# Instruction order at three places of a two-layer trunk, and a root kept in PSUM

## The chip, the cores and the metric

The kernel runs on one core of a Trainium2 chip. The core has a matrix engine (TensorE, PE), a vector engine (VectorE, DVE), a scalar engine (ScalarE, ACT), a general engine (GpSimd, POOL) and an engine that only issues transfers (SyncE, SP). Each works through a queue of its own in order, and they meet at semaphores. The metric is the device time of one execution in microseconds, as the median of several runs.

## The reference

Two layers are applied to 1024 prompt frames and 32 sample frames of width 1024, all in float32. Each layer has a recurrent mixer and a feed-forward part with a convolution over three frames; layer 0 has retention, layer 1 has gated linear attention (GLA).

```python
def rmsnorm(x, g):
    y = x * lax.rsqrt(jnp.mean(x * x, axis=-1, keepdims=True) + EPS)
    return y * g

def gla_chunk(S, xs):                  # q, k, v and the log decay lg of a chunk
    b = jnp.cumsum(lg, axis=1)
    expo = where(causal, b[:, :, None] - b[:, None, :], -inf)
    A = einsum('bihd,bjhd,bijhd->bhij', q, k, exp(expo))
    intra = einsum('bhij,bjhe->bihe', A, v)
    cross = einsum('bihd,bhde->bihe', q * exp(b), S)
    S_new = exp(bL) * S + einsum('bjhd,bjhe->bhde', k * exp(bL - b), v)

def gla_mixer(h, S0, w_in, w_a2, b_a, norm_g, w_out):
    q, k, v, r, a = split(h @ w_in)    # a: 16 decay features per frame
    lg = log_sigmoid(a @ w_a2 + b_a) / GLA_TAU
    ...
    return (silu(r) * o) @ w_out

def conv_ffn(h, conv_state, w_up, conv_w, conv_b, w_down):
    u = h @ w_up                       # 2 * 2816 columns
    c = conv_b + sum(ext[:, j:j + T] * conv_w[j] for j in range(3))
    gate, val = split(c)
    return (silu(gate) * val) @ w_down

def trunk(x, ...):
    for i in range(2):
        x = x + mixer_i(rmsnorm(x, norm_mix[i]))
        x = x + conv_ffn(rmsnorm(x, norm_ffn[i]))
    return rmsnorm(x, norm_final)      # and the new states
```

## The kernel before

**Products.** Features lie on the 128 partitions (eight tiles `kt`), the 1056 frames along the columns. A float32 product is made of three TensorE matmuls: the operand is split into a high part and the rest, and high x high, high x rest and rest x high are added in PSUM. `load_w` (L103) does this for a weight tile of 128x1024: a transfer into `raw`, a cast by ScalarE to `whi`, and a subtraction by VectorE to `wlo` (both at L110). `raw` has three buffers, so the next load waits for these two. `split_x` (L160) does it for the activations: ScalarE writes `xh` (XA in the trace, L162), VectorE `xl` (L163).

**The down projection**, the class `Down7`, works on 22 tiles of the 2816 columns in windows. The frames are in two halves `s` of 528 columns, each of two blocks of 264 (TH). A 2x2 block product is made with seven products instead of eight (`product`; ORD is the order of the seven, and L1703 to L1705 are the three matmuls of a term). VectorE adds each result from its PSUM tile `pu` into the residual `AR`: at L1784 after the seven products, at L1720 for the last windows, which are plain (`plain_product`). A PSUM tile can be written again only after these adds. The four row groups `p` of the residual become final one after the other.

**Behind the last windows.** In layer 0 `new_squares` adds the squares of the new residual into R (L1811), `new_x` splits it into `xh` and `xl` with the gain of the next norm and stores it, and `rms_a` and `rms_b` make the root of the mean for one chunk of columns: a matmul with ones gives the sums (`pn`, L189), ScalarE takes Ln and Exp, VectorE does a Newton step (L177 to L179) and writes the diagonal matrix `dg` (L196), and a matmul of `dg` with ones spreads the result over the partitions (`pr`, L202), from where ScalarE copies it into R. In layer 1 `squares`, `row`, `root` and `out` do the final norm for blocks (s, half): `row` sums the squares on TensorE (L1842) and issues Ln, Exp and a square on ScalarE, `root` is the Newton step on VectorE (L1853 to L1855), and four `out` per block multiply the residual by R (L1860) and store it.

**The GLA** has four heads and three chunks of 384, 384 and 288 columns. `gates_in(c)` makes the decay features, `qk_products` the products with the weights of q and k, `qk_out` scales them, `gate` makes the scan b along the columns, `weigh` the exponentials x at seven levels (GpSimd subtracts at L1116, ScalarE takes Exp, VectorE multiplies by k and q at L1122 and L1123). `scores` makes the mask A (L1171) and the scores (L1180), and `mix` the values with the weights `w_gv`, whose rest part is `vl` (L1262).

**What sets the order.** A scheduler places the instructions of each engine from the order of the calls and the waits; `order(a, b)` forces a behind b. The tables `ends` and `news` in `run` say behind which product (window, half, index) the steps of the end are called.

## Time and profile before

| | |
|---|---|
| Median of 3 timed runs | 2796.37 us (2794.09 to 2799.51) |
| The profiled execution | 2787.05 us, span 2785.3 us |
| Mean granted TensorE clock in it | 0.997 |
| TensorE busy | 2733.5 us, 98% |
| VectorE busy | 2047.1 us, 73% |
| ScalarE busy | 1370.3 us, 49% |
| GpSimd busy | 402.7 us, 14% |

The span is the time from the first to the last instruction of the execution; start times in the timelines count from its start. Busy time of an engine says nothing of what it holds up; that is read from the waits and the timeline. The end of layer 0 lies at about 1560 to 1585 us, the first scores of the GLA at 1622 us and the end of layer 1 behind 2757 us.

### The profile page before, as it was taken

How to read it: one execution, taken by the hardware profiler on the slowest of the kernel's cores; microseconds unless marked ns; L12 is line 12 of the kernel's file. 1: busy time of each engine (PE TensorE's matmuls, PEld its weight loads, DVE VectorE, ACT ScalarE, POOL GpSimd, SP SyncE). 2: the span in 40 equal slices, each digit the busy share in tenths (PEclk: the TensorE clock that was granted, in tenths of full speed). 3: DMA queues.
4: the chain of work that ended last, by engine and by line, in shares of the span. 5: the costliest groups of instructions: out<-in, count | busy, mean ns of one | idle time of the engine just before them, and what ended most of it. 6: DMA issues, size and time to landing. Idle time of an engine off the chain costs nothing.

```text
span 2785.3 us, 55419 instructions
## 1 busy us (share of the span) xinstructions
PE 2733.5 (98%) x22272; PEld 2644.8 (95%) x22272; DVE 2047.1 (73%) x3558; ACT 1370.3 (49%) x2520; POOL 402.7 (14%) x672
## 2 busy tenths in 40 slices
PE   9999999999999999999999889999999999999997
PEld 9999988888999999999999889999999999999997
DVE  7876666766557988888876777775379888888666
ACT  7444354444435544444544466664255444446445
POOL 0000000000112211111211232220132111112113
PEclk9999999999999999999999999999999999999999
DMA  6233455554875343323988411115532442329883
GB/s 241 87 115 102 137 157 139 160 143 117 287 252 186 118 141 124 104 96 111 299 200 227 147 32 53 54 46 199 184 128 93 138 141 101 108 82 306 200 223 115
DMA packets 276241, 410.30 MB, mean 147 GB/s; under 512 B 56784, under 2 KB 208976, under 8 KB 270864
## 3 DMA queue, kind: packets, MB, share of 16 engines
q1 hardware_dynamic: 257184, 347.88, 38.4%
q0 software_dynamic: 18256, 58.35, 8.8%
q8 instruction: 174, 2.85, 0.4%
q14 instruction: 83, 0.68, 0.1%
q10 hardware_dynamic: 544, 0.54, 0.1%
HBM read 264.49 MB, written 142.21 MB: 146 GB/s over the span
## 4 chain that ended last, share of the span: by engine, by line
PE 81%; DVE 7%; ACT 3%; DMA 3%; POOL 2%; issue 2%; SPq 0%; DVEq 0%; ACTq 0%; POOLq 0%
PE pu L436 13%; PE pu L431 13%; PE pu L435 13%; PE pu L1703 4%; PE pu L1704 4%; PE pu L1705 4%; PE pd L1513 2%; PE pd L1511 2%; PE pd L1512 2%; PE psv L265 2%; PE psv L266 2%; PE psv L267 2%; POOL x L1116 2%; PE pg L133 1%; PE pg L134 1%
## 5 line engine op out<-in xcount | busy, mean ns | idle before, releaser
L410 ACT COPY HR<-pu 128x264 f32<-128x264 f32 x264 | 98.7, 375 | 257.8 <-PE pu L436 251.8
L436 PE MATMUL pu<-XA,wgl 128*128 128x264 f32 x752 | 213.4, 284 | 0.0
L431 PE MATMUL pu<-XA,wgh 128*128 128x264 f32 x752 | 212.8, 283 | 0.0
L435 PE MATMUL pu<-XA,wgh 128*128 128x264 f32 x752 | 212.5, 283 | 0.0
L1987 DVE SCALAR_TENSOR_TENSOR AR<-AR,cw 128x1058 f32<-128x1058 f32 x88 | 115.9, 1319 | 70.8 <-ACT AR L1986 63.3
L1960 DVE TENSOR_TENSOR AR<-HR,pu 128x264 f32<-128x264 f32 (+2 forms) x440 | 144.2, 369 | 5.6 <-ACT HR L410 3.7
L431 PEld LDWEIGHTS pu<-XA,wgh 128*128 128x128 f32 x752 | 141.2, 188 | 0.3 <-ACT wgh L367 0.3
L435 PEld LDWEIGHTS pu<-XA,wgh 128*128 128x128 f32 x752 | 141.2, 188 | 0.0
L436 PEld LDWEIGHTS pu<-XA,wgl 128*128 128x128 f32 x752 | 141.0, 188 | 0.0
L431 PE MATMUL pu<-XA,wsh 128*128 128x264 f32 x464 | 132.5, 286 | 2.3 <-ACT HR L410 1.2
L436 PE MATMUL pu<-XA,wtl 128*128 128x264 f32 x464 | 131.9, 284 | 0.0
L436 PE MATMUL pu<-XA,wsl 128*128 128x264 f32 x464 | 131.8, 284 | 0.0
L431 PE MATMUL pu<-XA,wth 128*128 128x264 f32 x464 | 131.6, 284 | 0.0
L435 PE MATMUL pu<-XA,wsh 128*128 128x264 f32 x464 | 131.4, 283 | 0.0
L435 PE MATMUL pu<-XA,wth 128*128 128x264 f32 x464 | 131.1, 283 | 0.0
L1984 POOL COPY cst<-AR 128x2 f32<-128x2 f32 x88 | 49.8, 566 | 562.3 <-DVE AR L1960 562.3
L1986 ACT ACTIVATE AR<-AR,cw 128x1058 f32<-128x1058 f32 x88 | 111.8, 1273 | 12.2 <-DVE AR L1960 11.1
L1988 DVE SCALAR_TENSOR_TENSOR AR<-AR,cw 128x1058 f32<-128x1058 f32 x88 | 115.6, 1316 | 0.0
L110 DVE TENSOR_TENSOR wlo<-raw,whi 128x1024 fp32r<-128x1024 f32 x74 | 93.1, 1262 | 28.2 <-ACT whi L110 21.8
L110 ACT CAST whi<-raw 128x1024 fp32r<-128x1024 f32 x74 | 77.0, 1049 | 59.7 <-PE pg L134 25.3
L368 DVE TENSOR_TENSOR wtl<-rv,wth 128x1024 fp32r<-128x1024 f32 x58 | 70.9, 1223 | 41.3 <-ACT wth L367 41.0
L436 PE MATMUL pu<-XB,wtl 128*128 128x264 f32 x352 | 100.5, 286 | 0.0
(667 smaller groups left out, 11060.9 us busy)
## 6 DMA issues: line engine op xcount, KB each, us to landing
scr_h<-AR SPq DMA_DIRECT2D x162, 264.0 KB, 2.5
scr_x<-AR POOLq DMA_DIRECT2D x88, 264.0 KB, 6.7
rg<-w_up SPq DMA_DIRECT2D x44, 512.0 KB, 3.8
rv<-w_up SPq DMA_DIRECT2D x44, 512.0 KB, 3.6
raw<-w_ro SPq DMA_DIRECT2D x39, 512.0 KB, 5.8
XA<-scr_h SPq DMA_DIRECT2D x64, 264.0 KB, 5.0
AR<-scr_x SPq DMA_DIRECT2D x12, 1056.0 KB, 7.1
scr_hr<-hl SPq DMA_DIRECT2D x20, 512.0 KB, 4.1
```

The lines of the kernel that those rows point to most:

```text
L110: ins = S.copy(hi, raw), V.tensor_tensor(lo, raw, hi.bitcast(F32), op=ALU.subtract)
L410: ins = S.copy(t, b)
L431: mm = PE.matmul(ps, wh[:, k], x[:, 0, kt], start=m in (1, 2, 4, 5) and kt == 0, stop=False, skip_group_check=True)
L435: PE.matmul(ps, wh[:, k], x[:, 1, kt], start=False, stop=False, skip_group_check=True)
L436: mm = PE.matmul(ps, wl[:, k], x[:, 0, kt], start=False, stop=kt == 3, skip_group_check=True)
L1703: PE.matmul(ps, wh, x[:, 0], start=first, stop=False, skip_group_check=True)
L1704: PE.matmul(ps, wh, x[:, 1], start=False, stop=False, skip_group_check=True)
L1705: return PE.matmul(ps, wl, x[:, 0], start=False, stop=last, skip_group_check=True)
L1960: last_put[0] = V.tensor_tensor(u[:, d:d + n], t[:, o:o + n], b[:, o:o + n], op=op)
L1986: S.activation(cj, uj[:, 2:T + 4], AF.Identity, scale=cw[:, nt, 2:3], bias=cw[:, nt, 3:4])
L1987: V.scalar_tensor_tensor(cj, uj[:, 1:T + 3], cw[:, nt, 1:2], cj, op0=ALU.mult, op1=ALU.add)
L1988: V.scalar_tensor_tensor(cj, uj[:, 0:T + 2], cw[:, nt, 0:1], cj, op0=ALU.mult, op1=ALU.add)
```

## The change

It has three parts.

1. **End of layer 0, second half.** The weights `w_gqk` of the first head are loaded by a new method `ahead`, whose VectorE step is ordered behind the last add into the residual (`self.put`). The splits `new_x` of three row groups are called behind the last product and ordered behind that add as well. The root of chunk 0 is called at other products; `dg` and its product with ones are replaced by three matmuls of the root, broadcast along the columns, with the identity.
2. **Start of the GLA.** `gates_in` is cut in two (`gates_in`, `gates_out`) and uses the PSUM tag "lv". The sums of chunk 1 are called between the q and the k product of head 0, the roots of chunks 1 and 2 and the features follow in another order. The VectorE step of the first `w_gv` is ordered behind the features of chunk 2.
3. **End of layer 1.** `row` of block (1, 0) is called behind the last product. `root` writes its result over the PSUM tile, ScalarE copies it to R except for the last block, and `out` reads the PSUM tile on VectorE and R on GpSimd. One more `out` goes to GpSimd.

```diff
@@ -157,11 +157,13 @@
 
-    def split_x(idx, src, kt, c0, n):
+    def split_x(idx, src, kt, c0, n, after=None):
         g = gcol[:, idx, kt:kt + 1]
         ins = S.activation(xh[:, kt, c0:c0 + n], src, AF.Copy, scale=g)
-        V.scalar_tensor_tensor(xl[:, kt, c0:c0 + n], src, g, xh[:, kt, c0:c0 + n].bitcast(F32),
-                               op0=ALU.mult, op1=ALU.subtract)
+        lo = V.scalar_tensor_tensor(xl[:, kt, c0:c0 + n], src, g, xh[:, kt, c0:c0 + n].bitcast(F32),
+                                    op0=ALU.mult, op1=ALU.subtract)
+        if after is not None:
+            order(lo, after)
@@ -191,15 +193,20 @@
         V.tensor_scalar(m_, ps[:, 0:3], 1.0 / D, EPS, op0=ALU.mult, op1=ALU.add)
-        rsqrt(r_, t_, m_)
-        dg = nps[0].tile([P, 3, P], F32, tag="dg", name=f"dg{i}", bufs=1)
-        V.tensor_tensor(dg, ident.unsqueeze(1).to_broadcast([P, 3, P]),
-                        r_.unsqueeze(2).to_broadcast([P, 3, P]), op=ALU.mult)
-        return dg
-
-    def rms_b(dg, c, ps):
+        for ins in (S.activation(t_, m_, AF.Ln), S.activation(r_, t_, AF.Exp, scale=-0.5)):
+            order(ins, table[0])
+        return r_, t_, m_
+
+    def newton(r_, t_, m_):
+        V.tensor_tensor(t_, r_, r_, op=ALU.mult)
+        V.scalar_tensor_tensor(t_, t_, -0.5, m_, op0=ALU.mult, op1=ALU.mult)
+        return V.scalar_tensor_tensor(r_, t_, 1.5, r_, op0=ALU.add, op1=ALU.mult)
+
+    def rms_b(c, ps):
         c0, n = CM[c]
-        PE.matmul(ps[:, :n], ones, dg.rearrange("p m t -> p (m t)")[:, :n], start=True, stop=True)
+        for m, (o, _, L) in enumerate(minors(c)):
+            PE.matmul(ps[:, o:o + L], rc[:, 3 * c + m:3 * c + m + 1].to_broadcast([P, P]), ident[:, :L],
+                      start=True, stop=True)
@@ -1054,7 +1061,7 @@
 
-        def qk_products(h, c):
+        def qk_products(h, c, between=None):
@@ -1062,6 +1069,8 @@
             proj(pq[:, :n], wq[h], c0, n)
+            if between:
+                between()
@@ -1218,7 +1227,7 @@
             if c == 0:
-                wv[h] = [load_w(io["w_gv"][h, t], None, (None, second_mask[0])) for t in range(2)]
+                wv[h] = [load_w(io["w_gv"][h, t], None, (None, second_mask[0] or features[2])) for t in range(2)]
@@ -1345,10 +1354,14 @@
             c0, n = CM[c]
-            ps = pp.tile([P, 512], F32, tag="pj", name=f"pa{c0}", bufs=2)
+            ps = lv("pa")
             for kt in range(KT):
                 PE.matmul(ps[:32, :n], wa[:, kt], xh[:, kt, c0:c0 + n], start=kt == 0, stop=False)
                 PE.matmul(ps[:32, :n], wa[:, kt], xl[:, kt, c0:c0 + n], start=False, stop=kt == KT - 1)
+            return ps
+
+        def gates_out(c, ps):
+            c0, n = CM[c]
@@ -1357,18 +1370,26 @@
 
-        gates_in(0)
-        p00 = qk_products(0, 0)
+        def mean(c):
+            return rms_a(c, pp.tile([P, GDV], F32, tag="v", name=f"pn{uid()}", bufs=2))
+
+        g00 = gates_in(0)
+        mid = []
+        p00 = qk_products(0, 0, lambda: (gates_out(0, g00), mid.append(mean(1))))
+        newton(*mid[0])
         q00 = qk_out(0, p00)
+        rms_b(1, lv("pr"))
+        mid = mean(2)
         b00 = gate(0, 0)
-        for c in (1, 2):
-            rms_b(rms_a(c, lv("pn")), c, lv("pr"))
+        g01 = gates_in(1)
+        newton(*mid)
+        rms_b(2, lv("pr"))
+        gates_out(1, g01)
+        gates_out(2, gates_in(2))
         for f in closers:
             f()
         g2 = es.enter_context(pool("g2", side="right"))
         units = [(h, c) for h in range(GH) for c in range(3)]
-        gates_in(1)
-        gates_in(2)
@@ -1717,7 +1738,7 @@
                 y = self.Y[p][:, tile, t0 + half * TH:t0 + half * TH + TH]
-                V.tensor_tensor(y, y, ps, op=ALU.add)
+                self.put = V.tensor_tensor(y, y, ps, op=ALU.add)
@@ -1766,6 +1787,10 @@
 
+        def ahead(self, j):
+            k = self.nxt[j]
+            ahead[k] = load_w(io[k[0]][k[1:]], None, (None, self.put))
+
@@ -1814,7 +1839,7 @@
             for j in range(2):
-                split_x(2, y[:, j], 2 * p + j, t0, n)
+                split_x(2, y[:, j], 2 * p + j, t0, n, self.put if s else None)
@@ -1846,18 +1871,21 @@
                 order(ins, table[0])
-            self.rows[s, half] = m_, t_, r_, ps
+            self.rows[s, half] = ps, m_, t_, r_
 
         def root(self, s, half):
-            m_, t_, r_, ps = self.rows.pop((s, half))
+            ps, m_, t_, r_ = self.rows[s, half]
             V.tensor_scalar(m_, ps, 1.0 / D, EPS, op0=ALU.mult, op1=ALU.add)
             V.scalar_tensor_tensor(t_, t_, -0.5, m_, op0=ALU.mult, op1=ALU.mult)
-            V.scalar_tensor_tensor(r_, t_, 1.5, r_, op0=ALU.add, op1=ALU.mult)
+            V.scalar_tensor_tensor(ps, t_, 1.5, r_, op0=ALU.add, op1=ALU.mult)
+            if not (s and half):
+                S.copy(r_, ps)
 
         def out(self, s, half, q, eng=V):
             t0, n = 2 * TH * s + TH * half, TH
             y = self.Y[q][:, :, t0:t0 + n]
-            eng.tensor_tensor(y, y, R[:, t0:t0 + n].unsqueeze(1).to_broadcast([P, 2, n]), op=ALU.mult)
+            r = R[:, t0:t0 + n] if eng is G else self.rows[s, half][0]
+            eng.tensor_tensor(y, y, r.unsqueeze(1).to_broadcast([P, 2, n]), op=ALU.mult)
@@ -1887,19 +1915,19 @@
             got = {}
-            row, root, out = self.row, self.root, self.out
+            row, root, out, root_of = self.row, self.root, self.out, newton
             ends = {(0, 1): [(row, 0, 0)], (0, 2): [(root, 0, 0)], (0, 3): [(out, 0, 0, 3, G), (out, 0, 0, 0), (row, 0, 1)],
                     (0, 4): [(out, 0, 0, 1), (root, 0, 1)], (0, 5): [(out, 0, 0, 2)],
                     (0, 6): [(out, 0, 1, 3, G), (out, 0, 1, 0)], (1, 0): [(out, 0, 1, 1)], (1, 1): [(out, 0, 1, 2)],
-                    (1, 3): [(row, 1, 0)],
-                    (2, 3): [(root, 1, 0), (row, 1, 1)] + [(out, 1, 0, q) for q in (3, 0, 1, 2)]
+                    (2, 3): [(row, 1, 0), (root, 1, 0), (row, 1, 1), (out, 1, 0, 3, G)] + [(out, 1, 0, q) for q in range(3)]
                     + [(root, 1, 1)] + [(out, 1, 1, q) for q in (3, 0, 1, 2)]}
             new = self.new_x
-            dg = []
+            mean = []
             news = {(0, 0, 0): [(self.consts,)], (1, 0, 1): [(new, 3, 0)], (1, 0, 3): [(new, 0, 0)], (2, 0, 1): [(new, 1, 0)],
-                    (0, 1, 0): [(new, 2, 0)], (0, 1, 3): [(lambda: dg.append(rms_a(0, self.sm("pn"))),)],
-                    (0, 1, 5): [(lambda: rms_b(dg[0], 0, self.sm("pr")),)], (1, 1, 0): [(preload, *self.nxt)],
-                    (1, 1, 1): [(new, 3, 1)], (1, 1, 3): [(new, 0, 1)], (2, 1, 1): [(new, 1, 1)], (2, 1, 3): [(new, 2, 1)]}
+                    (0, 1, 0): [(new, 2, 0)], (0, 1, 2): [(lambda: mean.append(rms_a(0, self.sm("pn"))),)],
+                    (0, 1, 4): [(lambda: root_of(*mean[0]),)], (0, 1, 6): [(lambda: rms_b(0, self.sm("pr")),)],
+                    (1, 1, 0): [(self.ahead, 0)], (1, 1, 1): [(new, 3, 1)], (1, 1, 2): [(self.ahead, 1)],
+                    (2, 1, 3): [(new, 0, 1), (new, 1, 1), (new, 2, 1)]}
```

**VectorE, end of layer 0.** The rows around the first add from pu983, product 3 of the second half; pu981 and pu982 hold products before it, pu987 and on the plain windows at the end, wlo988 to wlo991 the rests of `w_gqk`. Before:

```order
L110 TENSOR_TENSOR wlo989_17466<-raw989_17463,whi989_17465 128x1024
L177 TENSOR_TENSOR tm985_17396<-rc_66 128x3
L1784 TENSOR_TENSOR AR0_7514<-AR0_7514,pu981_17345 128x528
L178 SCALAR_TENSOR_TENSOR tm985_17396<-tm985_17396 128x3
L163 SCALAR_TENSOR_TENSOR XA_64<-AR0_7514,gcol_67,XA_64 128x528
L179 SCALAR_TENSOR_TENSOR rc_66<-tm985_17396,rc_66 128x3
L1784 TENSOR_TENSOR AR0_7514<-AR0_7514,pu983_17372 128x264
```

After:

```order
L1809 TENSOR_TENSOR AR0_7514<-AR0_7514,pu982_17361 128x264
L1809 TENSOR_TENSOR AR0_7514<-AR0_7514,pu981_17345 128x528
L1809 TENSOR_TENSOR AR0_7514<-AR0_7514,pu983_17372 128x264 x2
L1741 TENSOR_TENSOR AR0_7514<-AR0_7514,pu987_17443 128x264
L110 TENSOR_TENSOR wlo988_17460<-raw988_17457,whi988_17459 128x1024
L1741 TENSOR_TENSOR AR0_7514<-AR0_7514,pu989_17463 128x264
L163 SCALAR_TENSOR_TENSOR XA_64<-AR0_7514,gcol_67,XA_64 128x528 x2
```

The casts and the splits (gcol) that stood between the adds now stand behind the add of pu987, the first of the plain windows.

**TensorE, the same place.** Before, product 3 (pu983) follows product 7 (pu981) at once:

```order
L1704 MATMUL pu981_17345<-XB0_7526,dwth964_17040 128x264
L1705 MATMUL pu981_17345<-XB0_7526,dwtl965_17041 128x264
L1703 MATMUL pu983_17372<-XA_64,dwsh961_17023 128x264
L1704 MATMUL pu983_17372<-XA_64,dwsh961_17023 128x264
L1705 MATMUL pu983_17372<-XA_64,dwsl962_17024 128x264
```

After:

```order
L1726 MATMUL pu981_17345<-XB0_7526,dwtl965_17041 128x264
L208 MATMUL pr986_17438<-ident_73,rc_66 128x128 x3
L1724 MATMUL pu987_17443<-XA_64,dph967_17077 128x264
L1725 MATMUL pu987_17443<-XA_64,dph967_17077 128x264
L1726 MATMUL pu987_17443<-XA_64,dpl968_17078 128x264
```

The three `pr` matmuls and six matmuls of pu987, of which three are shown, now stand ahead of pu983.

**VectorE, ahead of the first scores.** A is the mask that the scores need, ql, gSl and k belong to the first two chunks. Before:

```order
L1137 TENSOR_TENSOR ql_1020_17808<-e_1018_17804,qh_1019_17807 128x384
L1237 TENSOR_TENSOR gSl1161_18791<-gS1159_18788,gSh1160_18790 128x256
L1074 SCALAR_TENSOR_TENSOR k_1027_17878<-pj_1025_17851,R_65 128x384
L1088 TENSOR_SCALAR t2_1030_17884<-pj_1028_17880,ba_17576 128x384
L1091 TENSOR_TENSOR t2_1030_17884<-t2_1030_17884,t1_1029_17882 128x384
L1171 TENSOR_TENSOR A_1033_17928<-pa1032_17891,dmask_17578 128x384
```

After:

```order
L1146 TENSOR_TENSOR ql_1023_17808<-e_1021_17804,qh_1022_17807 128x384
L110 TENSOR_TENSOR wlo1044_17999<-raw1044_17996,whi1044_17998 128x1024
L110 TENSOR_TENSOR wlo1045_18005<-raw1045_18002,whi1045_18004 128x1024
L1246 TENSOR_TENSOR gSl1164_18791<-gS1162_18788,gSh1163_18790 128x256
L1083 SCALAR_TENSOR_TENSOR k_1030_17878<-pj_1028_17851,R_65 128x384
L1097 TENSOR_SCALAR t2_1033_17884<-pj_1031_17880,ba_17576 128x384
L1100 TENSOR_TENSOR t2_1033_17884<-t2_1033_17884,t1_1032_17882 128x384
L1180 TENSOR_TENSOR A_1036_17928<-pa1035_17891,dmask_17578 128x384
```

The two casts of `w_gv` (wlo1044, wlo1045) have come in ahead of A.

**VectorE, end of layer 1.** pn2357 and pn2362 before, pn2362 and pn2365 after are the row sums of blocks (1, 0) and (1, 1). Before:

```order
L1854 SCALAR_TENSOR_TENSOR rt2359_32325<-rt2359_32325,rm2358_32324 128x264
L1835 TENSOR_TENSOR HR1_22503<-HR1_22503 128x264
L1855 SCALAR_TENSOR_TENSOR R_65<-rt2359_32325,R_65 128x264
L1835 TENSOR_TENSOR HR1_22503<-HR1_22503 128x264
L1860 TENSOR_TENSOR AR1_22507<-AR1_22507,R_65 128x2x264 x4
L1853 TENSOR_SCALAR rm2363_32356<-pn2362_32354 128x264
L1854 SCALAR_TENSOR_TENSOR rt2364_32357<-rt2364_32357,rm2363_32356 128x264
L1855 SCALAR_TENSOR_TENSOR R_65<-rt2364_32357,R_65 128x264
L1860 TENSOR_TENSOR AR1_22507<-AR1_22507,R_65 128x2x264 x4
```

After:

```order
L1860 TENSOR_TENSOR HR1_22503<-HR1_22503 128x264 x2
L1878 TENSOR_SCALAR rm2363_32348<-pn2362_32346 128x264
L1879 SCALAR_TENSOR_TENSOR rt2364_32349<-rt2364_32349,rm2363_32348 128x264
L1880 SCALAR_TENSOR_TENSOR pn2362_32346<-rt2364_32349,R_65 128x264
L1878 TENSOR_SCALAR rm2366_32359<-pn2365_32357 128x264
L1888 TENSOR_TENSOR AR1_22507<-AR1_22507,pn2362_32346 128x2x264 x3
L1879 SCALAR_TENSOR_TENSOR rt2367_32360<-rt2367_32360,rm2366_32359 128x264
L1880 SCALAR_TENSOR_TENSOR pn2365_32357<-rt2367_32360,R_65 128x264
L1888 TENSOR_TENSOR AR1_22507<-AR1_22507,pn2365_32357 128x2x264 x4
```

Three of the first block's multiplications stay on VectorE, and they now stand behind the first row of the second block's root.

## The prediction

> **What bounds the kernel now.** The page comes first, then TensorE's waits, then the timeline at the three places that the change touches.
>
> ```profile
> span 2785.3 us, 55419 instructions
> PE 2733.5 (98%) x22272; PEld 2644.8 (95%) x22272; DVE 2047.1 (73%) x3558; ACT 1370.3 (49%) x2520; POOL 402.7 (14%) x672
> ```
>
> TensorE is busy for 98% of the span, so an edit is worth only what it takes out of the 2% in which TensorE waits, plus the end of the program behind its last matmul. The next rows (waiter, what it waited for, total us, times, longest) are the waits at the places of the change.
>
> ```profile
> PE pu L1703 <- DVE AR L1784: 5.4, 6, 3.1
> PE pn L1842 <- DVE HR L1835: 4.6, 2, 2.4
> PE pl L1180 <- DVE A L1171: 0.8, 1, 0.8
> PE ouu L1280 <- DVE vl L1262: 1.4, 1, 1.4
> ```
>
> All are waits for VectorE (DVE), so the question at each joint is what stands ahead in VectorE's queue. TensorE's timeline (start, us, ..., idle before) from the end of layer 0 to the first scores of the gated linear attention (GLA):
>
> ```profile
> 1564.56 0.40 PE L1703 MATMUL pu<-XA,dwv 128*128 128x264 f32 x1 [0.39 <-DVE AR L1784]
> 1570.50 0.39 PE L1703 MATMUL pu<-XA,dwsh 128*128 128x264 f32 x1 [3.10 <-DVE AR L1784]
> 1581.01 0.28 PE L1705 MATMUL pu<-XB,dp 128*128 128x264 f32 x1
> 1584.41 0.36 PE L1350 MATMUL pa<-XA,XG 128*32 128x384 f32 x1 [3.12 <-DVE AR L1720]
> 1602.32 0.91 PE L202 MATMUL pr<-dg,ones 128*128 128x384 f32 x2 [0.44 <-DVE dg L196]
> 1606.53 0.45 PE L133 MATMUL pj<-XA,whi 128*128 128x384 f32 x1 [0.87 <-DVE asr L1353]
> 1609.05 0.73 PE L202 MATMUL pr<-dg,ones 128*128 128x288 f32 x2 [1.73 <-DVE dg L196]
> 1622.32 0.91 PE L1180 MATMUL pl<-x 128*32 128x64 f32 x48 [0.81 <-DVE A L1171]
> ```
>
> Two waits of 3.1 us stand at the end of layer 0, and 0.44 + 0.87 + 1.73 + 0.81 = 3.85 us at the start of the GLA. The granted clock belongs to the price. In the table by stage the columns are window, length, PE, PEld, DVE, ACT and POOL busy, granted clock, DMA share, GB/s:
>
> ```profile
> 1570.00:1584.40 14.40, 10.80 (x83) 10.31 (x83) 11.75 (x19) 7.46 (x11) 5.97 (x4) 1.00 0.47 153
> 1584.40:1588.40 4.00, 3.98 (x16) 2.38 (x17) 3.11 (x5) 2.43 (x4) 0.77 (x1) 0.67 0.93 311
> 1609.40:1619.10 9.70, 9.70 (x48) 9.61 (x46) 6.05 (x18) 4.79 (x16) 0.00 (x0) 0.82 0.01 2
> ```
>
> The first 3.1 us wait left the clock at 1.00, and the second was followed by 4.00 us at 0.67, which cost 4.00 x 0.33 = 1.3 us. The three short waits were followed by 9.70 us at 0.82, which cost 9.70 x 0.18 = 1.75 us.
>
> **Joint 1, the end of layer 0.** VectorE's rows ahead of the two long waits:
>
> ```profile
> 1567.37 1.22 DVE L110 TENSOR_TENSOR wlo<-raw,whi 128x1024 fp32r<-128x1024 f32 x1 [0.29 <-ACT rc L175]
> 1568.59 0.70 DVE L1784 TENSOR_TENSOR AR<-AR,pu 128x528 f32<-128x528 f32 x1
> 1569.28 0.76 DVE L163 SCALAR_TENSOR_TENSOR XA<-AR,gcol,XA 128x528 fp32r<-128x528 f32 x1
> 1570.03 0.42 DVE L1784 TENSOR_TENSOR AR<-AR,pu 128x264 f32<-128x264 f32 x1
> 1578.27 2.34 DVE L110 TENSOR_TENSOR wlo<-raw,whi 128x1024 fp32r<-128x1024 f32 x1 [0.91 <-PE pu L1704]
> 1581.55 2.48 DVE L163 SCALAR_TENSOR_TENSOR XA<-AR,gcol,XA 128x528 fp32r<-128x528 f32 x2
> 1583.94 0.76 DVE L1720 TENSOR_TENSOR AR<-AR,pu 128x264 f32<-128x264 f32 x2
> ```
>
> TensorE stops at 1570.50 - 3.10 = 1567.40, because the PSUM bank of product 3 is freed only by the L1784 add at 1570.03. Ahead of that add stand a weight cast of 1.22 us and a split of 0.76 us, which no near matmul needs. The change puts both behind `self.put`. What stays ahead is the 528-column add and the 264-column add, 0.70 + 0.42 = 1.1 us after the last matmul of product 7. In that time TensorE now runs the three `pr` matmuls and six matmuls of product pu987 that the new order puts in front. Six cost 6 x 10.80/83 = 0.8 us, and the three `pr` matmuls lie between 0.3 us and the 0.91 us of the `pr` row above. I take 0.6 us, about what the two-pass matmul cost that they replace. So 1.4 us cover 1.1 us, and the whole 3.10 us goes. The 0.39 us wait stays, since the adds ahead of it do not move.
>
> The last product ends at 1581.01 + 0.28 = 1581.29. `gates_in(0)` waits 3.12 us there, because its bank "pj" is read by the adds at 1583.94, and ahead of these stand a cast of 2.34 us and two splits of 2.48 us. The change moves that cast to the first scores, moves the splits of the second half behind the last adds, and takes a bank of "lv", which is freed by the add of the last product but one. That wait goes as well; I leave 0.1 us. The six splits that move behind the adds are read first by `gates_in(1)`, with `gates_in(0)` and both products of head 0 in between; if that cover failed, they would cost up to 6 x 0.76 = 4.6 us there. In SP's queue the stores `scr_x` and the loads of the masks stay ahead, and the next loads of `w_gqk` and `w_gv` fall behind the casts at the scores. They serve head 1, whose first cast the trace has far later, so I count nothing for them:
>
> ```profile
> 1654.81 1.22 DVE L110 TENSOR_TENSOR wlo<-raw,whi 128x1024 fp32r<-128x1024 f32 x1
> ```
>
>
> `gates_in(0)` then starts 3.10 + 3.0 = 6.1 us earlier, and with no long wait ahead of it the 0.67 phase goes: 1.3 us more, 7.4 us in all.
>
> The Trainium skill has a rule on that last point ("TensorE: Matmul & The Clock Gate", section "Part 1: The HAM clock gate"): the array falls to half rate after an idle window of about 3.4 us, and the window runs freely, without regard to when the waiting began. The trace agrees as far as it goes, since of two waits of equal length one was followed by 0.67 and the other by 1.00.
>
> **Joint 2, the start of the GLA.** In TensorE's queue the short waits vanish, because the norm of columns 384 and on is computed between the two products of head 0 and the decay features come before the first scores. TensorE alone would reach the first scores at 1622.32 - 7.4 - 3.85 - 1.75 = 1609.3, and five value matmuls (0.6 us) move behind the scores: 1608.7. But VectorE must come there too.
>
> ```profile
> 1599.91 0.96 DVE L1093 TENSOR_TENSOR_SCAN b<-smask,t 128x384 f32<-128x384 f32 x1
> 1602.28 0.90 DVE L1122 TENSOR_TENSOR x<-x,k 128x192 f32<-128x192 f32 x1
> 1603.10 1.00 DVE L1123 TENSOR_TENSOR x<-x,q 128x192 f32<-128x192 f32 x1
> 1613.32 0.35 DVE L1122 TENSOR_TENSOR x<-x,k 128x192 f32<-128x192 f32 x1
> 1613.59 0.36 DVE L1123 TENSOR_TENSOR x<-x,q 128x192 f32<-128x192 f32 x1
> 1621.63 0.55 DVE L1171 TENSOR_TENSOR A<-pa,dmask 128x384 f32<-128x384 f32 x1
> 1601.01 6.40 POOL L1116 TENSOR_TENSOR x<-b 128x384 f32<-128x384 f32 x7 [13.46 <-DVE tm L178]
> ```
>
> The scan b ends at 1600.87. In the changed kernel it comes 7.4 us earlier, less 0.9 us for the second norm's matmuls that now stand ahead of it: 1594.4. Behind it VectorE has to do, before the mask A that the scores wait for: 1.4 us to the first product with x (as from 1600.87 to 1602.28); fourteen such products, seven beside GpSimd's 6.40 us at about 0.9 us and seven alone at 0.27 us from start to start, 6.3 + 1.9 = 8.2 us; twelve rows of the size of A (two pairs of features, e, kd, q, ql, k, two of the next gate and A itself) at some 0.48 us, 5.8 us; and the two `w_gv` casts that the change puts here, 2 x 1.2 = 2.4 us. That is 17.8 us, so A ends at 1612.2, against 1622.18 before: 10.0 us earlier. TensorE waits about 3.5 us for it. VectorE is the bound here, not TensorE.
>
> Behind the scores some is given back. The five value matmuls cost 0.6 us, and `vl` now stands behind two more products with x, 0.54 us alone and 1.9 us beside GpSimd; TensorE waited 1.4 us for `vl` already, so this is added in full. I take 1.2 us. Joints 1 and 2 together: 10.0 - 0.6 - 1.2 = 8.2 us.
>
> **Joint 3, the end.**
>
> ```profile
> 2761.66 0.40 PE L1703 MATMUL pu<-XA,dwsh 128*128 128x264 f32 x1 [0.88 <-DVE AR L1784]
> 2770.67 0.68 PE L1842 MATMUL pn<-HR,ones 128*128 128x264 f32 x2 [2.15 <-DVE HR L1835]
> 2775.24 0.71 PE L1842 MATMUL pn<-HR,ones 128*128 128x264 f32 x2 [2.42 <-DVE HR L1835]
> 2761.87 3.01 DVE L1860 TENSOR_TENSOR AR<-AR,R 128x528 f32<-128x528 f32 x2
> 2775.10 2.56 DVE L1860 TENSOR_TENSOR AR<-AR,R 128x528 f32<-128x528 f32 x4
> 2779.04 2.56 DVE L1860 TENSOR_TENSOR AR<-AR,R 128x528 f32<-128x528 f32 x4
> 2762.52 1.79 POOL L1860 TENSOR_TENSOR AR<-AR,R 128x528 f32<-128x528 f32 x1
> 2775.99 0.48 ACT L1846 ACTIVATE rt<-pn,epsc 128x264 f32<-128x264 f32 x1 [0.90 <-PE pn L1842]
> ```
>
> Row (1,0) no longer holds up the last products: its wait of 2.15 us and about 0.4 us of the 0.88 us go, and its own 0.68 us moves into the gap of 2.42 us. The last row matmul comes about 3.2 us earlier. But then both roots lie behind it. Before, the four multiplications of the first half (2.56 us) ran beside ScalarE's Ln, Exp and square of the second half (from 2775.99), and from 2775.24 to the end it was 2785.3 - 2775.24 = 10.1 us. Now ScalarE goes alternately through six activations and the copy of R, about 0.45 us each, so that the first half's multiplications start about 3.1 us behind the row. Three of them take 1.9 us, the second root's two rows 0.9 us, the last four 2.6 us, and 3.7 us follow the last VectorE row as before (2785.3 - 2781.6): 12.2 us. The joint gives 3.2 - 2.1 = 1.1 us. If the three run beside GpSimd's multiplication at 3.01/2 = 1.5 us each, they cost 2.6 us more and the joint loses 1.5 us; if the row comes 4 us earlier it gains 2. An operand in PSUM makes each product only as dear as the 0.70 us add of 1568.59 (0.64 us before), 0.4 us over seven. I take 1.0 us.
>
> Sum: 8.2 + 1.0 = 9.2 us. The profiled execution, 2787.05 us, would become 2777.9. It lies 9.3 us under the median of the timed runs, 2796.37; what separates them does not sit at these joints, so I forecast 2796.37 - 9.2 = 2787.2 us.
>
> **The rivals.** (a) VectorE swallows more at the scores: all fourteen products run beside GpSimd at 0.9 us, 12.6 us instead of 8.2. Then joints 1 and 2 give 3.8 us, and with 1.0 us the time is 2791.6. For it speaks that GpSimd's next rows follow the 6.40 us at once; against it, that the products from 1613.32 ran at 0.35 us.
>
> (b) The clock. The new wait of 3.5 us at the scores is followed by 4.00 us at 0.67, as the one before 1584.41 was, and 1.3 us are lost behind the scores: 2788.5 us. For it speaks that wait, against it the one before 1570.50, behind which the clock stayed at 1.00, and that the loss may hide under the wait for `vl`. The Trainium skill's page named above, same section, would have it happen, since its window is 3.4 us.
>
> (c) Slower: VectorE beside GpSimd the whole way from b to A. Fourteen products at 1.00 us, both casts at the 2.34 us of 1578.27, the rest 7.2 us: 25.9 us, and six splits at 1.24 us in front delay b by 2 us. A ends at 1622.3, no earlier than before. Behind it 0.6 + 1.9 us are given back and 1.3 us go to the clock; the tail loses 1.5 us by the same contention and 0.4 us to PSUM: 5.8 us slower, 2802.2. With those losses behind it, the change turns slower once b to A takes over 20 us. The order speaks against it: the casts stand where GpSimd has no work until the next scan, which is behind A.
>
> **How the numbers follow.** Forecast 0.66, (a) 0.16, (b) 0.07, (c) 0.11. A measurement can tell 0.2%, 5.6 us, from no change: faster means under 2790.8. The forecast's own ends are 1608.7 for A (TensorE's arrival, 3.5 us better) and two us each for `vl` and the tail, so 2782 to 2791; it is faster in nearly all of it, (b) is, (a) lies within 0.2% in three cases of four. Faster 0.75, same 0.14, slower 0.11. The range takes in (a) with the dear end of the tail (2.5 us) and of `vl` (1.3 us) and leaves out (c): 2781 to 2796.
>
> **What would show it.** In the changed profile the waits of 3.1 us before product 3 and `gates_in(0)` should be gone, with no clock under 0.9 behind them; one wait of 3 to 4 us for A should stand at the first scores, with two casts in VectorE's queue before it; the last row matmul should lie about 12 us from the end. If a wait at product 3 remains, the six filling matmuls are too few; if A comes after 1616 on this clock, GpSimd's contention was undersized.

## The result, and the profile after

| | before | after |
|---|---|---|
| Median of 5 runs each | 2794.09 us (2789.94 to 2799.51) | 2776.91 us (2775.37 to 2784.27) |
| Profiled execution, span | 2787.05 us, 2785.3 us | 2776.20 us, 2774.4 us |
| Mean granted TensorE clock | 0.997 | 0.997 |

The ratio is 0.9941 with an interval of 0.9923 to 0.9960: the changed kernel is faster by 16.5 us (11.2 to 21.5). The forecast was 2787.2 us, range 2781 to 2796. The sign is right, and the time lies 10.3 us under the forecast and 4.1 us under the range.

TensorE's timeline in the changed kernel (start, us, ..., idle before) shows the places of the prediction, and one wait that is new (1609.41):

```profile
1569.27 0.83 PE L208 MATMUL pr<-ident,rc 128*128 128x128 f32 x6
1570.69 0.39 PE L1724 MATMUL pu<-XA,dwsh 128*128 128x264 f32 x1
1580.75 0.36 PE L1359 MATMUL pa<-XA,XG 128*32 128x384 f32 x1 [0.66 <-DVE AR L1741]
1609.41 0.41 PE L1091 MATMUL pj<-XG 96*128 96x384 f32 x1 [0.87 <-DVE q L1081]
1614.61 0.91 PE L1189 MATMUL pl<-x 128*32 128x64 f32 x48 [2.65 <-DVE A L1180]
1624.05 0.38 PE L1289 MATMUL ouu<-vl,kh 128*128 128x256 f32 x1 [0.24 <-DVE vl L1271]
```

Both waits of 3.1 us are gone, and 0.66 us is left of the second. The wait for the mask A has grown from 0.8 to 2.65 us, as announced, but the wait for `vl` has shrunk from 1.4 to 0.24. Product 3 (1570.69) has no idle time in front of it: the `pr` matmuls and six of pu987 fill the gap. VectorE's rows show where the 0.66 us come from:

```profile
1574.62 3.24 DVE L163 SCALAR_TENSOR_TENSOR XA<-AR,gcol,XA 128x528 fp32r<-128x528 f32 x2
1578.12 1.21 DVE L110 TENSOR_TENSOR wlo<-raw,whi 128x1024 fp32r<-128x1024 f32 x1
1579.26 1.77 DVE L1741 TENSOR_TENSOR AR<-AR,pu 128x264 f32<-128x264 f32 x5
```

`self.put` is the add that is the last when a step is called, not the last of all. So the casts of `w_gqk` and the splits of row group 3 still stand among the plain adds, with five adds behind them. The table by stage (window, length, PE, PEld, DVE, ACT and POOL busy, granted clock, DMA share, GB/s) gives the clock:

```profile
1585.00:1592.00 7.00, 7.00 (x44) 7.00 (x43) 4.28 (x11) 1.44 (x4) 0.24 (x1) 1.00 0.23 73
1615.60:1619.00 3.40, 3.14 (x15) 2.94 (x16) 3.25 (x6) 2.92 (x11) 3.40 (x5) 0.51 0.07 22
```

The start of the GLA now runs at the full clock. But behind the wait for A stands one stretch of 3.4 us at half rate, which is what rival (b) described. VectorE between the scan and `vl`:

```profile
1596.72 0.96 DVE L1102 TENSOR_TENSOR_SCAN b<-smask,t 128x384 f32<-128x384 f32 x1
1601.68 0.98 DVE L1131 TENSOR_TENSOR x<-x,k 128x192 f32<-128x192 f32 x1
1607.52 0.34 DVE L1132 TENSOR_TENSOR x<-x,q 128x192 f32<-128x192 f32 x1
1609.66 2.35 DVE L110 TENSOR_TENSOR wlo<-raw,whi 128x1024 fp32r<-128x1024 f32 x2
1613.91 0.55 DVE L1180 TENSOR_TENSOR A<-pa,dmask 128x384 f32<-128x384 f32 x1
1623.52 0.47 DVE L1271 SCALAR_TENSOR_TENSOR vl<-pv,rc,vh 128x256 fp32r<-128x256 f32 x1
```

From the end of the scan (1597.68) to the end of A (1614.46) it is 16.8 us. The end of layer 1, TensorE, VectorE and GpSimd:

```profile
2759.56 0.61 PE L1867 MATMUL pn<-HR,ones 128*128 128x264 f32 x2
2761.43 0.71 PE L1867 MATMUL pn<-HR,ones 128*128 128x264 f32 x2 [1.25 <-DVE HR L1860]
2748.52 0.69 DVE L1888 TENSOR_TENSOR AR<-AR,pn 128x528 f32<-128x528 f32 x1
2751.72 1.31 DVE L1888 TENSOR_TENSOR AR<-AR,pn 128x528 f32<-128x528 f32 x2
2764.36 1.93 DVE L1888 TENSOR_TENSOR AR<-AR,pn 128x528 f32<-128x528 f32 x3
2748.54 1.34 POOL L1888 TENSOR_TENSOR AR<-AR,R 128x528 f32<-128x528 f32 x1 [1.90 <-ACT R L1882]
2753.97 3.02 POOL L1860 TENSOR_TENSOR HR<-HR 128x264 f32<-128x264 f32 x4
2764.40 1.30 POOL L1888 TENSOR_TENSOR AR<-AR,R 128x528 f32<-128x528 f32 x1 [4.32 <-ACT R L1882]
```

VectorE's multiplications with an operand in PSUM (`pn`) take 0.64 to 0.70 us each, although GpSimd multiplies at the same time. The same three groups before, from VectorE and GpSimd:

```profile
2757.17 2.46 DVE L1860 TENSOR_TENSOR AR<-AR,R 128x528 f32<-128x528 f32 x2
2757.21 1.85 POOL L1860 TENSOR_TENSOR AR<-AR,R 128x528 f32<-128x528 f32 x1 [1.43 <-DVE R L1855]
2765.75 3.77 POOL L1835 TENSOR_TENSOR HR<-HR 128x264 f32<-128x264 f32 x4 [1.44 <-ACT HR L1834]
```

With both operands in SBUF a multiplication took 2.46/2 = 1.23 us (1.5 in the prediction's row), GpSimd's took 1.85 us instead of 1.34, and its four squares 3.77 us instead of 3.02.

**Pieces.** Whole executions of one kernel differ by several us, so I also compare pieces of the traces, cut at the same VectorE instructions. These cut the piece of joints 1 and 2, first before, then after (an add shortly before the end of layer 0, and a `vl` behind the first scores):

```profile
1517.56 0.42 DVE L1761 TENSOR_TENSOR AR<-AR,pu 128x264 f32<-128x264 f32 x1
1679.77 0.48 DVE L1262 SCALAR_TENSOR_TENSOR vl<-pv,rc,vh 128x256 fp32r<-128x256 f32 x1
```

```profile
1519.91 0.42 DVE L1782 TENSOR_TENSOR AR<-AR,pu 128x264 f32<-128x264 f32 x1
1671.93 0.47 DVE L1271 SCALAR_TENSOR_TENSOR vl<-pv,rc,vh 128x256 fp32r<-128x256 f32 x1
```

162.21 us became 152.02, so joints 1 and 2 gave 10.2 us in these two executions. The last piece runs from an add behind the last products (2740.47 before, 2731.34 after) to the end of the span: 44.8 us became 43.1, so joint 3 gave 1.7 us. All the rest, which the change does not touch, was 1.1 us longer after than before.

### The profile page after: what moved, and what is told of

Read it like the earlier page. It is cut to its first block, busy times and chain, and to the rows that moved or that the text cites. A ratio compares the mean times of both kernels' runs of the same rounds, so it can differ in the third digit from the quotient of the medians.

```text
span 2774.4 us, 55430 instructions
## 1 busy us (share of the span) xinstructions
PE 2732.4 (98%) x22284; PEld 2645.4 (95%) x22284; DVE 2041.7 (74%) x3554; ACT 1370.4 (49%) x2523; POOL 398.7 (14%) x673
## 4 chain that ended last, share of the span: by engine, by line
PE 47%; DVE 5%; DMA 3%; ACT 3%; POOL 2%; issue 2%; SPq 0%; DVEq 0%; ACTq 0%; POOLq 0%
PE pu L443 8%; PE pu L438 8%; PE pu L442 8%; PE pu L1724 4%; PE pu L1725 4%; PE pu L1726 4%; POOL x L1125 2%; PE pg L133 1%; PE pg L134 1%; PE pg L135 1%; DMA dg<-w_down 1%; PE pv L272 1%; PE pv L273 1%; PE pv L274 1%; DMA dv<-w_down 1%
## 5 line engine op out<-in xcount | busy, mean ns | idle before, releaser
L110 DVE TENSOR_TENSOR wlo<-raw,whi 128x1024 fp32r<-128x1024 f32 x74 | 91.2, 1239 | 30.1 <-ACT whi L110 25.0
```

Of the source, the lines that this page charges most:

```text
L110: ins = S.copy(hi, raw), V.tensor_tensor(lo, raw, hi.bitcast(F32), op=ALU.subtract)
```

## The experiments

All pieces below are in us against the first profile of the kernel before; "rest" is the sum of the other pieces, the same code in every kernel. Each is one profiled execution.

| kernel | joints 1 and 2 | end | rest |
|---|---|---|---|
| after | -10.2 | -1.7 | +1.1 |
| after again | -10.2 | -1.7 | +0.3 |
| before again | -0.7 | +0.4 | +4.6 |
| joints 1 and 2 only | -10.2 | +0.6 | +6.1 |
| joint 3 only | +0.5 | -1.7 | +2.2 |
| after, root in R | -8.7 | +2.3 | +0.4 |
| before, root in PSUM | +3.8 | -3.5 | +6.0 |
| joint 1 only | -6.5 | +0.4 | +2.6 |
| splits unordered | -9.9 | -1.7 | +7.0 |
| value casts unordered | -10.4 | -1.7 | +5.5 |
| value casts early | -12.1 | -1.7 | +6.3 |
| row back | -8.7 | -3.6 | +1.4 |
| row back, casts early | -12.0 | -3.6 | +7.0 |

In three executions, of "after, root in R", "row back" and "before, root in PSUM", the granted clock just behind the first cut (1518 to 1526 us) was 0.79 instead of 1.00, behind waits of TensorE of 1.99, 1.76 and 2.67 us ahead of the cut. This accounts for the 1.5 us that the first two lack (-8.7 against -10.2), since their code there is that of the changed kernel. About as much of the +3.8 of the third has the same source, which lies ahead of the joints.

**After again, and before again.** No edit.

> The changed kernel once more, on the chip of the other three runs. Theory A (the gain is what the two traces show at the three joints, 10.2 us at the first two and 3.6 us at the end, 13.8 us in all; the rest of the 17 us between the medians is scatter between runs): the timed difference lies at 12 to 15 us. Theory B (something outside the joints gains as well): 16 to 18 us again.

> The kernel before, profiled once more. If the 7 us between its first profiled execution and its median are scatter along the whole program, the piece from 1518 to 1679 us (joints 1 and 2) and the piece from 2647 us to the end keep their lengths within 1 us, and the rest is longer by several us. If the waits at the joints cost more in an ordinary run (more half-rate windows of the clock), these two pieces are longer.

After: 2778.26 us (2775.38 to 2781.12, 6 runs), the kernel before beside it 2794.33 (2787.57 to 2799.37, 17 runs), ratio 0.9951 (0.9937 to 0.9964), which is 13.7 us (10.1 to 17.6); the medians themselves are 16.1 us apart. So the times do not decide between the two theories. In the table the rest averages 3.2 us over the four executions with the old first two joints and 3.8 us over the ten others: no gain outside the joints shows. (The 3.6 us at the end, in this and the next expectations, were read from a piece that began at 2647 us; 1.9 us of them lie ahead of 2740 us.) Before again, one run: 2791.32 us. Its two pieces agree with the first profile within 0.7 us, and its rest is 4.6 us longer. So the differences between executions are made along the whole program, and do not come from the joints alone.

**The two halves of the change.** Joints 1 and 2 only is the changed kernel with `row`, `root`, `out` and the table `ends` of before. Joint 3 only is the kernel before with these four as changed.

> Joints 1 and 2 alone, with the end of layer 1 as before. By the traces 10.2 us faster than the kernel before, with no change behind 1640 us; by the prediction 8.2 us. If the joints depend on each other (an earlier GLA changes the end), the end would move too and the sum with the next run would not be that of the whole.

> Joint 3 alone on the kernel before. By the traces 3.6 us faster, by the prediction 1.0 us. With e2 the sum should be 13 to 14 us, if the joints are independent.

Joints 1 and 2 only: 2782.87 us, ratio 0.9964 (0.9951 to 0.9976), 10.1 us. Joint 3 only: 2792.01 us, ratio 0.9993 (0.9984 to 1.0002), 2.0 us, with an interval that takes in zero. The two add up to the whole within the intervals, in the pieces and in the times. In the rows of joint 3 only, the old waits stand before product 3 and `gates_in(0)`:

```profile
1572.99 0.59 PE L1703 MATMUL pu<-XA,dwsh 128*128 128x264 f32 x1 [3.10 <-DVE AR L1784]
1589.39 0.53 PE L1350 MATMUL pa<-XA,XG 128*32 128x384 f32 x1 [3.12 <-DVE AR L1720]
```

**What joint 3 consists of.** The joint does two things: it moves `row` of block (1, 0) (and with it one `out`) behind the last product, and it leaves the root in PSUM. In "after, root in R" only the second is undone, in "before, root in PSUM" only the second is done.

```diff
 # after, root in R
-            V.scalar_tensor_tensor(ps, t_, 1.5, r_, op0=ALU.add, op1=ALU.mult)
-            if not (s and half):
-                S.copy(r_, ps)
+            V.scalar_tensor_tensor(r_, t_, 1.5, r_, op0=ALU.add, op1=ALU.mult)
...
-            r = R[:, t0:t0 + n] if eng is G else self.rows[s, half][0]
-            eng.tensor_tensor(y, y, r.unsqueeze(1).to_broadcast([P, 2, n]), op=ALU.mult)
+            eng.tensor_tensor(y, y, R[:, t0:t0 + n].unsqueeze(1).to_broadcast([P, 2, n]), op=ALU.mult)
```

> The changed kernel with the root written to R as before and all multiplications reading R; the order of row, root and out at the end, with one more multiplication on GpSimd, stays as changed. Theory P (the PSUM operand is the gain: VectorE's multiplications no longer run at half speed beside GpSimd's): the multiplications beside GpSimd take 1.2 to 1.5 us each again instead of 0.65, the waits before product 3 and the last rows come back, and most of the 3.6 us is lost. Theory M (moving row (1, 0) behind the last product is the gain): at most 1 us is lost.

2781.92 us, ratio 0.9962 (0.9949 to 0.9975). Its VectorE and GpSimd rows and its last two rows on TensorE:

```profile
2748.84 2.46 DVE L1885 TENSOR_TENSOR AR<-AR,R 128x528 f32<-128x528 f32 x2
2748.89 1.85 POOL L1885 TENSOR_TENSOR AR<-AR,R 128x528 f32<-128x528 f32 x1 [1.43 <-DVE R L1880]
2769.29 2.92 DVE L1885 TENSOR_TENSOR AR<-AR,R 128x528 f32<-128x528 f32 x3
2769.11 1.29 POOL L1885 TENSOR_TENSOR AR<-AR,R 128x528 f32<-128x528 f32 x1 [4.29 <-DVE R L1880]
2757.42 3.79 POOL L1860 TENSOR_TENSOR HR<-HR 128x264 f32<-128x264 f32 x4 [1.44 <-ACT HR L1859]
2762.27 0.71 PE L1867 MATMUL pn<-HR,ones 128*128 128x264 f32 x2 [0.63 <-DVE HR L1860]
2766.17 1.10 PE L1867 MATMUL pn<-HR,ones 128*128 128x264 f32 x2 [3.19 <-DVE HR L1860]
```

The slow multiplications and squares are back to within 0.02 us, TensorE waits 3.19 us for the last row instead of 1.25, and the end is 4.0 us longer than in the changed kernel and 2.3 us longer than before. The new order alone loses. About 1.0 us of this is its one more multiplication on GpSimd, beside which VectorE's three take 2.92 us; with the root in PSUM they took 1.93.

The kernel before with the root in PSUM:

> The kernel before with one edit of joint 3: the root is written over its PSUM tile, ScalarE copies it to R except for the last block, and VectorE's multiplications read PSUM. Row (1, 0) and the number of multiplications on GpSimd stay as before. If the PSUM operand is what counts, VectorE's multiplications beside GpSimd's take 0.65 to 0.7 us instead of 1.23 and 1.5, the wait of 0.88 us before the last window's product 3 goes, and most of the 3.5 us at the end is there. If the order counts, less than 1 us.

One run, 2793.30 us. TensorE's rows of the sums and VectorE's last multiplications:

```profile
2777.06 0.71 PE L1842 MATMUL pn<-HR,ones 128*128 128x264 f32 x2
2781.22 0.71 PE L1842 MATMUL pn<-HR,ones 128*128 128x264 f32 x2 [1.99 <-DVE HR L1835]
2781.37 2.55 DVE L1863 TENSOR_TENSOR AR<-AR,pn 128x528 f32<-128x528 f32 x4 [0.20 <-ACT R L1857]
2785.30 2.54 DVE L1863 TENSOR_TENSOR AR<-AR,pn 128x528 f32<-128x528 f32 x4
```

Row (1, 0), left in its old place, waits for nothing (2.15 us before): its squares arrive in time. From the last row to the end it is 2791.5 - 2781.22 = 10.3 us (10.1 before). The end gains 3.5 us, twice what the whole joint gave. So the PSUM operand carries the joint, and moving the row takes about half of its gain back. That the whole run shows nothing of it is the doing of the first piece and the rest (+3.8 and +6.0 us).

**What joint 1 consists of.** Joint 1 only has the start of the GLA in the order of before, the old end and no order on the `w_gv` casts:

> Joint 1 without joints 2 and 3: the order of the end of layer 0 as changed, the start of the GLA in the order of before (with the bank lv for the features and the roots by the new products), the casts of w_gv unordered as before. By the prediction's working the two waits of 3.1 us go, 6 us at the first product of the GLA; the short waits of the GLA's start (0.44, 0.87, 1.73 us) stay or grow, and the first scores come 6 to 8 us earlier than before instead of 10.

One run, 2783.44 us; the piece gave 6.5 us. The wait before product 3 is gone, but, against the expectation, the wait for the bank of `gates_in(0)` is still 2.27 us. The next two edits tell why. The first sets the splits `new_x` back to their old places without an order, the second takes the order off the first `w_gv` casts:

```diff
 # splits unordered
-                split_x(2, y[:, j], 2 * p + j, t0, n, self.put if s else None)
+                split_x(2, y[:, j], 2 * p + j, t0, n)
-                    (2, 1, 3): [(new, 0, 1), (new, 1, 1), (new, 2, 1)]}
+                    (1, 1, 3): [(new, 0, 1)], (2, 1, 1): [(new, 1, 1)], (2, 1, 3): [(new, 2, 1)]}
 # value casts unordered
-wv[h] = [load_w(io["w_gv"][h, t], None, (None, second_mask[0] or features[2])) for t in range(2)]
+wv[h] = [load_w(io["w_gv"][h, t], None, (None, second_mask[0])) for t in range(2)]
```

> The changed kernel with new_x of the second half at its old products and not ordered behind the last adds; the weight casts stay behind them. By the prediction's working a split of 0.76 us in front of the adds before product 3 and two splits of 1.24 us in front of the last adds come back: the first still hides under the filling matmuls in part (wait up to 0.5 us), at the first product of the GLA a wait of 1 to 2.5 us stands instead of 0.66. If the casts alone were the cause, no wait over 0.8 us.

One run, 2782.43 us. Against the expectation, the wait of `gates_in(0)` grew only from 0.66 to 0.86 us, and product 3 did not wait:

```profile
1583.59 0.37 PE L1359 MATMUL pa<-XA,XG 128*32 128x384 f32 x1 [0.86 <-DVE AR L1741]
```

The splits slip between the adds and hold up a bank by 0.2 us. Holding them back is worth some 0.3 us (-9.9 against -10.2, one execution); the next run shows what the casts are worth.

> The changed kernel without the order that holds the first w_gv casts behind the features of chunk 2: one cast goes between the last adds of layer 0, the other ahead of the features of chunk 0. By VectorE's rows the first delays the bank that the features wait for by 1.2 us (wait 1.9 instead of 0.66 us), the second is hidden, and A comes about 1 us earlier than in the changed kernel, since 2.35 us have left its queue.

One run, 2780.47 us. VectorE's first `w_gv` cast, then TensorE's rows at `gates_in(0)`, A and `vl`:

```profile
1579.25 1.66 DVE L110 TENSOR_TENSOR wlo<-raw,whi 128x1024 fp32r<-128x1024 f32 x1
1581.64 0.36 PE L1359 MATMUL pa<-XA,XG 128*32 128x384 f32 x1 [2.26 <-DVE AR L1741]
1613.65 0.91 PE L1189 MATMUL pl<-x 128*32 128x64 f32 x48 [0.81 <-DVE A L1180]
1623.11 0.39 PE L1289 MATMUL ouu<-vl,kh 128*128 128x256 f32 x1 [1.60 <-DVE vl L1271]
```

Unordered, one of the two casts stands among the last adds (the other comes at 1587.24 us, behind them) and TensorE waits 2.26 us for its bank; ordered, both stand ahead of A and TensorE waits 2.65 us there. Counted from the first cut, A comes only 0.2 us earlier than in the changed kernel, not 1 us. The piece is the same within 0.2 us (-10.4 and -10.2). The order on `w_gv` moves the wait and gains nothing.

**The casts where neither wait is.** The first `w_gv` is loaded and cast behind the Newton step of chunk 1:

```diff
-        newton(*mid[0])
+        nw = newton(*mid[0])
         q00 = qk_out(0, p00)
+        for t in range(2):
+            ahead["w_gv", 0, t] = load_w(io["w_gv"][0, t], None, (None, nw))
...
-                wv[h] = [load_w(io["w_gv"][h, t], None, (None, second_mask[0] or features[2])) for t in range(2)]
+                wv[h] = [weights("w_gv", h, t, after=(None, second_mask[0])) for t in range(2)]
```

> The changed kernel with the two w_gv casts moved from just ahead of the first mask A to behind the Newton step of chunk 1, where VectorE waited 2.4 us for TensorE. If VectorE's queue is what holds the first scores, A comes 2.3 us earlier, TensorE's wait for it shrinks from 2.6 us to under 0.5, and the whole gains about 2 us. If TensorE or the clock is behind the wait, under 0.5 us.

2778.39 us (2774.74 to 2779.52, 5 runs), ratio 0.9943 (0.9929 to 0.9956). TensorE's rows at A and `vl` are those of the run before, to 0.01 us. The wait for A falls from 2.65 to 0.81 us (under 0.5 was expected), and no half-rate stretch follows it (the clock from 1560 to 1630 us is 1.00). But `vl` is then waited for again, 1.60 us instead of 0.24. Net, the piece gives 1.9 us more than the changed kernel; the timed runs do not show it.

**Row back, and both.** `(1, 3): [(row, 1, 0)]` is put back into `ends`; then this and the early casts together, the best version that the pieces point to.

> The changed kernel with row (1, 0) back behind product (1, 3), everything else as changed (root in PSUM, one more multiplication on GpSimd). In the piece from 2740 us (of the kernel before) to the end the changed kernel gained 1.7 us and the root in PSUM alone 3.5 us. If moving the row is what lost the difference, this piece gains 3.5 to 4 us against the kernel before, and the whole is 2 us faster than the changed kernel. If not, it gains 1.7 us as the changed one.

> e9 with the w_gv casts behind the Newton step of chunk 1 as in e8. If the pieces are independent: 12.1 us less from 1518 to 1679 us and 3.5 to 4 us less from 2740 us to the end, 16 us in all against the kernel before, 4 us against the changed kernel, so 2773 to 2776 us as a median.

Row back: 2776.22 us (2774.10 to 2782.86, 5 runs), ratio 0.9942 (0.9930 to 0.9955); the end gives 3.6 us, as with the root in PSUM alone, but the 2 us that were expected against the changed kernel do not show in the time. Both: 2777.68 us (2777.28 to 2783.82, 5 runs), ratio 0.9948 (0.9934 to 0.9961). Its two pieces give 12.0 and 3.6 us, 15.6 against 11.9 in the changed kernel, and yet its time cannot be told from that of the changed kernel. In its profile the rest took 7.0 us more than in the first profile of before; one place of that is in layer 1 (VectorE, then TensorE):

```profile
2703.83 0.56 DVE L1704 TENSOR_TENSOR dv<-dv 128x384 f32<-128x384 f32 x1 [8.91 <-DMA dv<-w_down]
2704.79 0.39 PE L1726 MATMUL pu<-XB,dwsh 128*128 128x264 f32 x1 [2.79 <-DVE AR L1784]
```

VectorE waited 8.91 us for the load of a weight tile, `dv`, and the add that frees TensorE's bank stands behind that row. In the changed kernel the same two waits were 6.34 and 0.22 us, in the first profile of before 7.82 and 1.69, in joints 1 and 2 only 9.99 and 3.87: TensorE's wait grows by what VectorE's grows. So when this load lands is part of what makes the rest differ. A gain of 3.6 us at the joints is shown in the pieces; a better time of the whole is not shown.

## Why the prediction was off

**Joint 1: right.** `gates_in(0)` was to start 6.1 us earlier. The changed kernel was 2.35 us behind at the first cut (1519.91 against 1517.56); its first row of `gates_in(0)` came at 1580.75 instead of 1584.41, so it gained 2.35 + 3.66 = 6.0 us. The cover of 1.4 us for product 3 held (1570.69 - 1569.27 = 1.42 us). The parts fit less well than the sum: the second wait gave 3.12 - 0.66 = 2.5 us instead of 3.0, and where the 0.39 us wait was to stay, TensorE waited 0.96 us for the squares of chunk 0 (at 1565.20 us). The reason given for the wait at `gates_in(0)`, casts and splits ahead of the adds, was half right: it is 2.26 us with the `w_gv` casts unordered but only 0.86 with the splits unordered, against 0.66 in the changed kernel. What the other bank does ("lv" for "pj"), no run shows by itself.

**The mask A: right, in part by luck.** It was to end 10.0 us earlier and does so by 1622.18 + 2.35 - 1614.46 = 10.1 us. The products with x took 0.98 us beside GpSimd and 0.34 alone, so rival (a) did not happen, nor (c): 16.8 us from the scan to A, not over 20. But two errors cancel: the scan ended 0.9 us later than forecast (1597.68 - 2.35 = 1595.3 against 1594.4), and from there to A it took 1.0 us less than the 17.8 of the sum. TensorE was to wait 3.5 us and waited 2.65, because it too came 0.9 us late: not all the short waits vanished, the 0.87 us at 1609.41 is new.

**The give-back behind the scores: mis-sized.** The step "Joints 1 and 2 together: 10.0 - 0.6 - 1.2 = 8.2 us" was 2.0 us too small. Two rows of before, VectorE's `vl` and TensorE's wait behind the scores of the second chunk, show where:

```profile
1630.51 0.47 DVE L1262 SCALAR_TENSOR_TENSOR vl<-pv,rc,vh 128x256 fp32r<-128x256 f32 x1
1645.66 0.70 PE L1180 MATMUL pl<-x 128*32 128x64 f32 x33 [0.26 <-DVE gss L1319]
1647.02 0.44 PE L1180 MATMUL pl<-x 128*32 128x64 f32 x15 [0.66 <-issue]
```

From A to `vl` VectorE took 1630.51 - 1621.63 = 8.9 us before and 1623.52 - 1613.91 = 9.6 us after: `vl` came 0.7 us later behind A, where I had 1.2. I had added the five value matmuls (0.6 us) on top. They cost nothing, nor did the half-rate stretch: both lie in front of `vl`, where TensorE had 1.44 us to spare, of which 0.24 are left. In the two runs with early or unordered casts, whose clock stayed at 1.00, the wait for `vl` was 1.60 us. So rival (b) did come, but hidden, as its own "against" had allowed. That is 1.1 us of the 2.0. The other 0.9 us is a gain that I had not foreseen: the two waits at the second scores, 0.26 + 0.66 us, are not in the changed kernel.

The Trainium skill ("TensorE: Matmul & The Clock Gate", section "Part 1: The HAM clock gate") gives about 3.4 us as the idle window behind which the array falls to half rate. Here the stretch at half rate is 3.4 us long, as the page would have it, but the wait ahead of it was only 2.65 us. In the kernel before, the 9.70 us at 0.82 came behind a wait of 1.73 us.

**The clock of the kernel before: taken from one execution.** The price of 1.3 us for the phase behind 1584.41 was read from a window that ended too early: from 1585.74 to 1589.15 us the clock was 0.50, which costs 1.7 us. And the same 3.1 us waits were followed by other amounts of half rate in other executions. 70 us of the place, one row each for before, before again, joint 3 only and before with the root in PSUM, each in the table by stage:

```profile
1560.00:1630.00 70.00, 58.37 (x515) 52.06 (x513) 52.58 (x96) 37.30 (x89) 21.09 (x24) 0.95 0.22 70
```

```profile
1560.00:1630.00 70.00, 58.78 (x522) 52.53 (x521) 52.30 (x98) 35.89 (x84) 20.81 (x22) 0.95 0.23 74
```

```profile
1560.00:1630.00 70.00, 58.76 (x514) 52.24 (x513) 51.56 (x96) 35.22 (x82) 19.80 (x22) 0.93 0.23 75
```

```profile
1560.00:1630.00 70.00, 58.80 (x498) 51.66 (x497) 49.91 (x93) 33.39 (x75) 17.81 (x19) 0.90 0.23 76
```

The clock is 0.95, 0.95, 0.93 and 0.90, and the pieces are 0.0, -0.7, +0.5 and +3.8 us: the mean of the four is +0.9. Without the 1.5 us of the last that lie ahead of the joints it is +0.5. In the changed kernel, after again and joints 1 and 2 only it is 0.98 each time, and the pieces agree within 0.03 us. So the first two joints gave some 10.2 + 0.5 = 10.7 us on average over these executions.

**Joint 3: the sign right, the reason missed.** The step "an operand in PSUM makes each product only as dear as the 0.70 us add of 1568.59, 0.4 us over seven" counted the operand as a small loss, and contention with GpSimd as the dear end. The root in PSUM removes that contention, on both engines: 3.5 us alone, 4.0 us within the change. The order, which I had counted as the gain, loses 1.8 us with the root in PSUM, and 2.3 us with the root in R and the added multiplication on GpSimd. The pieces of the sum were nearer: from the last row to the end it is 2774.4 - 2761.43 = 13.0 us (12.2 forecast; 4.7 us follow VectorE's last row, where I had 3.7 as before), and the row lies 30.1 us behind the cut instead of 34.8 (2775.24 - 2740.47), 4.7 us earlier (3.2 forecast). The joint gave 1.7 us, or 2.1 against the mean of the four executions with the old end (+0.3 on average), where 1.0 was forecast.

The Trainium skill ("SBUF — State Buffer", section "Who interferes with whom") says that a VectorE instruction with two SBUF inputs contends with a GpSimd instruction that reads SBUF, and one with at most one SBUF input does not. The rows agree: 1.23 against 0.65 us. They also fit the two engines taking turns: VectorE's first multiplication (0.64), GpSimd's (1.30) and VectorE's second (0.64) add up to 2.6 us, near the 2.46 that VectorE's two took. I had not weighed this rule.

**The base: 2.3 us.** The step "2796.37 - 9.2" took a median of three runs for the level of the kernel. Five runs gave 2794.09 us, 17 others 2794.33.

**What adds up.** The pieces give 10.7 + 2.1 = 12.8 us. The second comparison measured 13.7 us (10.1 to 17.6) and the first 16.5 (11.2 to 21.5); both contain 12.8. That the first is 3.7 us above it is within what such a comparison can tell, and no cause of it is shown. The forecast of 2787.2 became 2776.9 by 2.3 us of the base, 3.6 us of the joints' sizes (12.8 - 9.2: 2.5 us in the step of the give-back, with the clock of the kernel before, and 1.1 us in that of the operand in PSUM) and 4.4 us whose cause stays open. With the base and the joints put right the sum gives 2781.3 us, just inside the range. The range held the unknown costs of the edits; it left out what a median of three or five runs leaves open, and what the clock behind long waits does in other executions.

## What to carry to other kernels

Look at an elementwise row of VectorE that runs beside GpSimd: if both its operands are in SBUF and one comes out of a step that could leave it in PSUM, leaving it there can be worth more than the reordering around it: here it gained 3.5 us, and the reordering lost 1.8. When a cast is moved out of one wait, follow it to the next place: ordered here or there it cost the same until it stood where TensorE waited for nothing. Where executions differ by more than the gain that is looked for, cut the traces at the same instructions and compare the pieces, and take the base and the clock's behaviour from several executions.
